# Two gaps in SBUF: weight tiles and gated activations moved to 224 bytes past a multiple of 256

## The chip, the core and the metric

The kernel runs on one core of a Trainium2 chip. The metric is the time of one execution in device microseconds (us). A run of the profiler gives, for one execution, the start and the duration of every instruction on the engines: TensorE (PE, and PEld for its weight loads), VectorE (DVE), ScalarE (ACT), GpSimd (POOL) and the queue of SyncE (SP), which issues the transfers from HBM.

## The reference

Two transformer stacks follow each other on x of 512 tokens by 1024 features, in float32. Most of the work is in the feed-forward layers and the projections:

```python
def swiglu(h, w_gu, w_d):
    g, u = jnp.split(h @ w_gu, 2, axis=-1)
    return (jax.nn.silu(g) * u) @ w_d
...
    for i in range(DEPTH):            # first block: 2 layers
        x = x + 0.5 * mx[2] * swiglu(modulate(rms_norm(x, norm_g[i, 0]), mx[0], mx[1]), ffn1_w_gu[i], ffn1_w_d[i])
        if ctx_in_layer:              # layer 0: 256 tokens of context y beside x
            y = y + 0.5 * my[2] * swiglu(modulate(rms_norm(y, norm_g[i, 0]), my[0], my[1]), ffn1_w_gu[i], ffn1_w_d[i])
...
        x = x + mx[5] * ox            # differential attention (i = 0) or Fourier mixing (i = 1)
        x = x + 0.5 * mx[8] * swiglu(modulate(rms_norm(x, norm_g[i, 2]), mx[6], mx[7]), ffn2_w_gu[i], ffn2_w_d[i])
...
    for l in range(DEPTH):            # second block: 2 layers
        mix = jnp.concatenate([o_a, o_b, o_c, o_d], axis=-1) @ w_out[l]
        h = layer_norm(DEEPNORM_ALPHA * h + mix, ln_mix_g[l], ln_mix_b[l])
        up = depthwise_conv(h @ ffn_w_up[l], ffn_conv_w[l], ffn_conv_b[l])
        f = (jax.nn.silu(up[..., :D_FF]) * up[..., D_FF:]) @ ffn_w_down[l]
        h = layer_norm(DEEPNORM_ALPHA * h + f, ln_ffn_g[l], ln_ffn_b[l])
```

The hidden width D_FF is 2816, that is 22 tiles of 128.

## The kernel before

Features lie on the 128 partitions and tokens along the free dimension, so an activation of 1024 features is a tile of 8 rows of 512 tokens in each partition. To keep float32 accuracy, every operand of a large product is split into two float32r numbers, a high and a low part, and a product is made of three matmuls: high weights by low activations, high by high, low by high. The helper `mm3` (L246 to L255) issues them, each loop of `product` one k-tile of 128 features:

```python
for pt, rh, rl in outs:
    self.PE.matmul(pt, lh, rl, start=start, stop=False)
for pt, rh, rl in outs:
    self.PE.matmul(pt, lh, rh, start=False, stop=False)
for pt, rh, rl in outs:
    last = self.PE.matmul(pt, ll, rh, start=False, stop=stop)
```

The first operand (`lh`, `ll`) is the stationary one, 128 by 128, which a weight load puts into the array; the second (`rl`, `rh`) is the moving one, which streams through it, 512 or 256 columns of 4 bytes in each partition. In a row of the profile `mm<-H,wh` the first name behind the arrow is the moving tile and the second the stationary one.

A unit of weights (512 KB, 4096 bytes in each partition) goes this way: SP issues its transfer into one of three raw tiles `wr` (L218), ACT copies it as float32r into `wh` and DVE makes the rest `wl` (L222 and L223, four tiles of each), then PE uses `wh` and `wl` for 24 matmuls or more. In the feed-forward layers the weights are stationary and the normed input `H` is moving (gate and up products), then the gated activations `ah` and `al`, which ACT and DVE split from `act` in the same way, are moving (down products, `into_stream`). In the projections that give tokens on partitions the roles are turned: `H` is stationary and `wh`, `wl` are moving. In the first feed-forward layer each matmul of 512 columns for x (bank `mm`) is followed by one of 256 columns for y (bank `my`) with the same weights. When a layer ends, the last four row blocks are made in two halves of 256 columns each, so that the norm of one half can begin during the other. In the mixers of the second block the attention scores are float32r matmuls of `q` and `k` with 512 columns (L1120, L1134 to L1136).

Nothing in the kernel chooses an address. Tiles lie in the order in which pools are opened: from the low end the pool `const`, then `weights` (`wr`, `wh`, `wl`), then `small` (tiles of 32 bytes), then the pools of a phase (`ah`, `al`, `act`, `t`, `q`, `k` and others); from the high end, on the right side, `H` and `Y`. Each tile takes its bytes in a partition, rounded up to 32. From the sizes this gives, as offsets in a partition modulo 256: `wr`, `wh`, `wl` 192 (the pool begins at 40640), `ah`, `al`, `act`, `q`, `k` and the attention outputs `Oh`, `Ol` 32 (the phases begin at 86816), `H` 224, `X` 192. Rows of a tile are whole multiples of 256 bytes apart, so all rows of one tile have its value, except for a few odd sizes in the Fourier phase.

Of the kernel before, what the change touches and what calls it, by code (L numbers as in the profile page):

```python
# [10 lines left out]
F32 = mybir.dt.float32  # L11
# [7 lines left out]
P = 128  # L19
# [45 lines left out]
class Seg:  # L65


    def __init__(self, x, lo, w, off, cond):
        self.x, self.lo, self.w, self.off, self.cond = x, lo, w, off, cond
# [103 lines left out]
class Net:  # L173
    def __init__(self, tc, a, out, ctx):
        self.tc, self.nc, self.a, self.out, self.ctx = tc, tc.nc, a, out, ctx
        nc = tc.nc
        self.V, self.S, self.G, self.PE = nc.vector, nc.scalar, nc.gpsimd, nc.tensor
        self.n = 0
        pool = lambda name, **k: ctx.enter_context(tc.tile_pool(name=name, **k))
        self.cp = pool("const", bufs=1)  # L180
        self.wp = pool("weights", bufs=1)
        self.sp = pool("small", bufs=1)
        self.fillers, self.done, self.ready = [], set(), {}
        self.steps, self.pending = 0, []

# [158 lines left out]
    def setup(self):  # L344
        nc, cp, a = self.nc, self.cp, self.a
        self.vec = cp.tile([P, NVEC], F32, name="vec")
        nc.sync.dma_start(self.vec, a["vecs"])
        self.X = cp.tile([P, KD, T], F32, name="X")
        self.ident = cp.tile([P, P], F32, name="ident")
        make_identity(nc, self.ident)  # L350
        self.ones = cp.tile([P, 2, 32], F32, name="ones")
        nc.vector.memset(self.ones, 0.0)
        for c in range(2):
            nc.vector.memset(self.ones[:, c, c:c + 1], 1.0)
        self.one2, self.ones = self.ones, self.ones[:, 0]
        self.row1 = self.one2[:, 0, :1]
        self.mhalf = cp.tile([P, 1], F32, name="mhalf")
        nc.vector.memset(self.mhalf, -0.5)
        self.eps = {e: cp.tile([P, 1], F32, name=f"eps{i}") for i, e in enumerate((1e-6, 1e-5))}
        for e, t in self.eps.items():  # L360
            nc.vector.memset(t, e)
        self.SC = cp.tile([P, KD, 32], F32, name="SC")
        nc.vector.memset(self.SC, 0.0)
        self.S.activation(self.SC[:, :, 0], self.v("c"), AF.Silu)
        self.S.activation(self.SC[:, :, 1], self.v("c_ctx"), AF.Silu)
        self.mod = [cp.tile([P, 9, KD, 2], F32, name=f"mod{l}") for l in range(2)]
        self.rows = cp.tile([P, 384], F32, name="rows")
        self.subg = cp.tile([P, 1], F32, name="subg")
        self.V.tensor_scalar(self.subg, self.v("sub_g"), 1.0 - LAMBDA_INIT, None, ALU.mult)
# [1169 lines left out]
```

## Time and profile before

| | |
|---|---|
| median of 3 runs | 3479.23 us (3478.27 to 3481.52) |
| profiled execution | 3478.89 us, span of its instructions 3477.1 us |
| mean granted TensorE clock | 0.991 of full speed |
| PE busy | 3371.0 us, 97% of the span |
| DVE, ACT, POOL busy | 1929.3, 1273.7, 318.9 us |
| from HBM | 336.82 MB, 97 GB/s over the span |

The profiled execution lies 0.34 us below the median. Matmuls are pipelined: the duration that the profile gives for one overlaps the next, so the pace of a stream of matmuls is read from starts, as the time from one start to a later one divided by the number of matmuls between them.

### The profile page before, as it was taken

What the parts mean: (1) busy time and instruction counts of PE and PEld (TensorE: products, weight loads), DVE (VectorE), ACT (ScalarE), POOL (GpSimd) and SP (SyncE); (2) the same over time, 40 slices, a digit from 0 to 9 for tenths busy, and PEclk for the clock granted to TensorE, in tenths of its full rate; (3) what the DMA queues carried; (4) which work ended last, traced back from release to release, by engine and by line L of the source; (5) the groups of instructions that cost most, each with busy time, mean ns of one, the idle gap of its engine ahead of it and who ended that gap; (6) DMA issues with size and microseconds to landing.
All of it is one profiled execution on the core that took longest, in us unless ns stands there. A gap on an engine that the chain in (4) does not pass through costs nothing.

```text
span 3477.1 us, 43820 instructions
## 1 busy us (share of the span) xinstructions
PE 3371.0 (97%) x17412; PEld 2785.0 (80%) x17412; DVE 1929.3 (55%) x2994; ACT 1273.7 (37%) x2197; POOL 318.9 (9%) x344
## 2 busy tenths in 40 slices
PE   6999999999999999999999999999999999999998
PEld 5888888777787777888888888886888888688887
DVE  6554444565855545433365333678645467865555
ACT  3212112436742222422244222445533344553333
POOL 1000000222210000100030000310100022010001
PEclk9999999999999999999999999999999999999999
DMA  6434443124235654323222322211222222023232
GB/s 214 136 112 124 131 133 98 61 72 108 58 123 175 197 160 158 101 93 93 90 88 86 96 92 93 93 52 36 86 91 91 96 92 69 25 85 94 90 100 63
DMA packets 105046, 352.51 MB, mean 101 GB/s; under 512 B 12037, under 2 KB 15237, under 8 KB 104585
## 3 DMA queue, kind: packets, MB, share of 16 engines
q1 hardware_dynamic: 104840, 349.71, 32.2%
q8 instruction: 137, 2.24, 0.3%
q14 instruction: 69, 0.56, 0.1%
HBM read 336.82 MB, written 2.10 MB: 97 GB/s over the span
## 4 chain that ended last, share of the span: by engine, by line
PE 43%; DVE 4%; ACT 1%; POOL 1%; issue 1%; DVEq 0%; ACTq 0%; POOLq 0%
PE mm L250 13%; PE mm L254 13%; PE mm L252 13%; PE tr L1144 1%; DVE ya L1252 1%; DVE nm L1121 0%; PE tr L285 0%; ACT H L222 0%; PE tr L290 0%; PE mm L1134 0%; PE mm L1153 0%; ACT X L166 0%; DVE t L164 0%; DVE t L165 0%; PE mm L1136 0%
## 5 line engine op out<-in xcount | busy, mean ns | idle before, releaser
L222 ACT ACTIVATE wh<-wr 128x1024 fp32r<-128x1024 f32 (+4 forms) x505 | 510.6, 1013 | 1397.9 <-PE mm L252 937.2
L250 PE MATMUL mm<-H,wh 128*128 128x512 f32 (+1 forms) x2592 | 970.9, 375 | 7.3 <-DVE H L138 3.0
L252 PE MATMUL mm<-H,wh 128*128 128x512 f32 (+1 forms) x2592 | 968.0, 374 | 0.0
L254 PE MATMUL mm<-H,wl 128*128 128x512 f32 (+1 forms) x2592 | 966.8, 374 | 0.2 <-DVE wl L223 0.2
L223 DVE TENSOR_TENSOR wl<-wr,wh 128x1024 fp32r<-128x1024 f32 (+4 forms) x505 | 595.7, 1182 | 472.4 <-ACT wh L222 461.5
L250 PEld LDWEIGHTS mm<-H,wh 128*128 128x128 f32 x2592 | 489.9, 189 | 107.6 <-issue 4.1
L254 PEld LDWEIGHTS mm<-H,wl 128*128 128x128 f32 x2592 | 489.5, 189 | 93.7 <-DVE wl L223 0.4
L252 PEld LDWEIGHTS mm<-H,wh 128*128 128x128 f32 x2592 | 490.5, 189 | 92.3
L250 PE MATMUL mm<-al,wh 128*128 128x512 f32 (+1 forms) x1216 | 445.0, 366 | 0.0
L252 PE MATMUL mm<-ah,wh 128*128 128x512 f32 (+1 forms) x1216 | 444.5, 366 | 0.0
L254 PE MATMUL mm<-ah,wl 128*128 128x512 f32 (+1 forms) x1216 | 443.1, 365 | 0.0
L250 PEld LDWEIGHTS mm<-al,wh 128*128 128x128 f32 x1216 | 228.2, 188 | 43.2 <-issue 1.2
L254 PEld LDWEIGHTS mm<-ah,wl 128*128 128x128 f32 x1216 | 228.7, 188 | 40.8
L252 PEld LDWEIGHTS mm<-ah,wh 128*128 128x128 f32 x1216 | 228.5, 188 | 40.1
L303 POOL TENSOR_TENSOR s<-s,mhalf 128x2 f32<-128x2 f32 (+4 forms) x70 | 77.7, 1110 | 1578.2 <-ACT s L310 815.8
L404 DVE SCALAR_TENSOR_TENSOR macc<-wr,SC,macc 128x1024 f32<-128x1024 f32 x133 | 168.5, 1281 | 90.8 <-DMA wr<-w_mod 90.2
L553 DVE SCALAR_TENSOR_TENSOR X<-mm,ng,X 128x512 f32<-128x512 f32 (+1 forms) x120 | 81.4, 678 | 246.3 <-PE mm L254 246.2
L513 DVE TENSOR_TENSOR act<-act,mm 128x512 f32<-128x512 f32 x88 | 60.4, 686 | 247.2 <-PE mm L254 247.1
L250 PE MATMUL mm<-wl,H 128*128 128x512 f32 (+2 forms) x480 | 178.2, 374 | 8.1 <-DVE wl L223 4.7
L254 PE MATMUL mm<-wh,H 128*128 128x512 f32 (+2 forms) x480 | 175.3, 367 | 0.3
L252 PE MATMUL mm<-wh,H 128*128 128x512 f32 (+2 forms) x480 | 174.9, 365 | 0.0
L222 ACT ACTIVATE ah<-act 128x512 fp32r<-128x512 f32 (+1 forms) x132 | 88.0, 667 | 161.5 <-DVE act L541 110.1
(351 smaller groups left out, 4323.4 us busy)
## 6 DMA issues: line engine op xcount, KB each, us to landing
wr<-gu SPq DMA_DIRECT2D x176, 512.0 KB, 3.5
wr<-w_mod SPq DMA_DIRECT2D x136, 512.0 KB, 4.2
wr<-up SPq DMA_DIRECT2D x88, 512.0 KB, 3.5
wr<-dn SPq DMA_DIRECT2D x48, 448.0 KB, 3.3
wr<-down SPq DMA_DIRECT2D x32, 448.0 KB, 3.3
wr<-qkv SPq DMA_DIRECT2D x24, 512.0 KB, 3.6
wr<-dn SPq DMA_DIRECT2D x24, 512.0 KB, 3.5
wr<-w_out SPq DMA_DIRECT2D x16, 512.0 KB, 3.6
```

Source lines behind the costliest of these rows:

```text
L222: self.S.activation(hi, src, AF.Copy)
L223: (eng or self.V).tensor_tensor(lo, src, hi.bitcast(F32), ALU.subtract)
L250: self.PE.matmul(pt, lh, rl, start=start, stop=False)
L252: self.PE.matmul(pt, lh, rh, start=False, stop=False)
L254: last = self.PE.matmul(pt, ll, rh, start=False, stop=stop)
L303: G.tensor_tensor(dst, v, self.mhalf.to_broadcast([P, w]), ALU.pow)
L404: self.V.scalar_tensor_tensor(acc[c], raw, s, acc[c], ALU.mult, ALU.add)
L513: self.V.tensor_tensor(to, to, pu, ALU.mult)
L553: self.V.scalar_tensor_tensor(s(d), pt, gate[0][:, d, s.cond:s.cond + 1], s(d), ALU.mult, ALU.add)
L1144: PE.matmul(d["o"], d["v"][:, t], d.pop(("p", t)), start=t == 0, stop=t == 3)
L1252: self.V.scalar_tensor_tensor(ya[:, j], ap[:, j, t:t + T], wt, ya[:, j], ALU.mult, ALU.add)
```

## The change

Two tiles are added that nothing writes or reads: one of 32 bytes in `const`, ahead of `SC`, and one of 160 bytes at the head of `small`.

```diff
@@ -180,6 +180,7 @@
         self.cp = pool("const", bufs=1)
         self.wp = pool("weights", bufs=1)
         self.sp = pool("small", bufs=1)
+        self.sp.tile([P, 40], F32, name="pad", tag="pad", bufs=1)
         self.fillers, self.done, self.ready = [], set(), {}
         self.steps, self.pending = 0, []
 
@@ -359,6 +360,7 @@
         self.eps = {e: cp.tile([P, 1], F32, name=f"eps{i}") for i, e in enumerate((1e-6, 1e-5))}
         for e, t in self.eps.items():
             nc.vector.memset(t, e)
+        cp.tile([P, 8], F32, name="gap")
         self.SC = cp.tile([P, KD, 32], F32, name="SC")
         nc.vector.memset(self.SC, 0.0)
         self.S.activation(self.SC[:, :, 0], self.v("c"), AF.Silu)
```

Everything behind `SC` in `const` and the pool `weights` move up by 32 bytes, everything from the small tiles on by 192. On every engine the same instructions stand in the same order with the same waits; only addresses differ. Offsets in a partition modulo 256:

| tiles | before | after |
|---|---|---|
| `wr`, `wh`, `wl` | 192 | 224 |
| `ah`, `al`, `act`, `q`, `k`, `Oh`, `Ol` | 32 | 224 |
| `H` (right side) | 224 | 224 |
| `X` | 192 | 192 |
| `ks`, `aT`, `pp` of the attention core | 64 | 0 |

## Rows read from the trace of the kernel before

**Rows 1.** The page, busy time: busy us (share of the span) xinstructions.

```profile
PE 3371.0 (97%) x17412; PEld 2785.0 (80%) x17412; DVE 1929.3 (55%) x2994; ACT 1273.7 (37%) x2197; POOL 318.9 (9%) x344
```

**Rows 2.** The waits: engine and line, waited for whom, us in total, times, longest.

```profile
ACT wh L222 <- PE mm L252: 938.5, 315, 5.9
```

**Rows 3.** The waits of SP's queue, in the same columns.

```profile
SPq L218 <- DVE wl L223: 2396.0, 465, 82.4
```

**Rows 4.** Groups by line and shape: xcount | busy us, mean ns | idle before, releaser.

```profile
L250 PE MATMUL mm<-H,wh 128*128 128x512 f32 x2080 | 824.0, 396 | 2.1 <-ACT wh L222 2.1
...
L222 ACT ACTIVATE wh<-wr 128x1024 fp32r<-128x1024 f32 x376 | 397.6, 1060 | 998.4 <-PE mm L252 712.1 <-PE my L252 140.0 <-DMA wr<-gu 76.8
L250 PE MATMUL mm<-al,wh 128*128 128x512 f32 x896 | 354.1, 396 | 0.0
...
L250 PE MATMUL mm<-H,wh 128*128 128x256 f32 x512 | 146.9, 290 | 5.2 <-DVE H L138 3.0 <-POOL H L223 1.7 <-DVE H L223 0.3
...
L250 PE MATMUL mm<-wl,H 128*128 128x512 f32 x320 | 127.9, 403 | 4.9 <-DVE wl L223 4.7
...
L250 PE MATMUL my<-H,wh 128*128 128x256 f32 x352 | 99.4, 282 | 0.0
...
L250 PE MATMUL mm<-al,wh 128*128 128x256 f32 x320 | 90.9, 284 | 0.0
...
L250 PE MATMUL my<-al,wh 128*128 128x256 f32 x176 | 49.3, 280 | 0.0
```

**Rows 5.** Timeline of PE, `H` moving, 512 columns: start us, us, instruction.

```profile
2000.07 0.40 PE L250 MATMUL mm<-H,wh 128*128 128x512 f32 x1
...
2039.98 0.39 PE L250 MATMUL mm<-H,wh 128*128 128x512 f32 x1
```

**Rows 6.** Timeline of PE, gated activations moving, 512 columns.

```profile
1939.88 0.40 PE L250 MATMUL mm<-al,wh 128*128 128x512 f32 x1
...
1979.78 0.40 PE L250 MATMUL mm<-al,wh 128*128 128x512 f32 x1
```

**Rows 7.** Timeline of PE, weights moving, 512 columns.

```profile
632.05 0.40 PE L250 MATMUL mm<-wl,H 128*128 128x512 f32 x1
...
659.81 0.40 PE L254 MATMUL mm<-wh,H 128*128 128x512 f32 x1
```

**Rows 8.** Timeline of PE, `H` moving, pairs of 512 and 256 columns.

```profile
364.77 0.39 PE L254 MATMUL mm<-H,wl 128*128 128x512 f32 x1
...
394.93 0.39 PE L254 MATMUL mm<-H,wl 128*128 128x512 f32 x1
```

**Rows 9.** Timeline of PE, gated activations moving, pairs of 512 and 256 columns.

```profile
314.76 0.39 PE L250 MATMUL mm<-al,wh 128*128 128x512 f32 x1
...
344.86 0.39 PE L254 MATMUL mm<-ah,wl 128*128 128x512 f32 x1
```

**Rows 10.** Timeline of PE, gated activations moving, 256 columns.

```profile
1375.85 0.29 PE L252 MATMUL mm<-ah,wh 128*128 128x256 f32 x1
...
1386.41 0.28 PE L254 MATMUL mm<-ah,wl 128*128 128x256 f32 x1
```

**Rows 11.** Timeline of PE, `H` moving, 256 columns, in two layers.

```profile
1403.87 0.28 PE L254 MATMUL mm<-H,wl 128*128 128x256 f32 x1
...
1419.96 0.28 PE L252 MATMUL mm<-H,wh 128*128 128x256 f32 x1
...
1851.84 0.28 PE L250 MATMUL mm<-H,wh 128*128 128x256 f32 x1
...
1869.96 0.28 PE L252 MATMUL mm<-H,wh 128*128 128x256 f32 x1
```

**Rows 12.** Timeline of PE, attention scores of the two mixers, 512 columns.

```profile
2386.76 0.40 PE L1134 MATMUL mm<-q,k 128*128 128x512 f32 x1
...
2388.14 0.38 PE L285 MATMUL tr<-ident,nm 128*128 128x128 f32 x2
...
3006.66 0.40 PE L1134 MATMUL mm<-q,k 128*128 128x512 f32 x1
...
3008.05 0.38 PE L285 MATMUL tr<-ident,nm 128*128 128x128 f32 x2
```

## The prediction

> **What bounds the kernel now.** I read the busy times first, because a change of addresses alone can only act through the durations of instructions and transfers. PE is busy 97% of the span [rows 1], so a change in the pace of its matmuls reaches the end nearly whole. Next come the waits, to see whether the feeders have room. ACT, which starts the split of each weight unit, stands 938.5 us waiting for PE to give back a `wh` tile [rows 2], and the queue that issues the weight transfers waits 2396.0 us for DVE to give back a raw tile [rows 3]. Both are ahead of PE, so a split or a transfer that became some per cent slower would be covered, and a faster PE is still fed.
>
> Then the groups by shape give the counts. `mm3` issues three matmuls a k-tile, on three lines with equal counts, so each L250 row stands for three. With 512 columns these are 3 × 2080 = 6240 with `H` moving, 3 × 896 = 2688 with the gated activations moving and 3 × 320 = 960 with weights moving. With 256 columns they are 3 × 512 = 1536 with `H` and 3 × 320 = 960 with gated activations, besides 3 × 352 = 1056 and 3 × 176 = 528 in bank `my`, nearly all of which follow a 512-column matmul as the second of a pair [rows 4].
>
> Last, the pace, from starts in the timeline. This is the reading that the whole forecast hangs on, since operands at different offsets modulo 256 already stand beside each other in this trace. I write (moving, stationary) for the two offsets.
> - 512 columns, (224, 192): 171 matmuls in 39.91 us, 233.4 ns each [rows 5].
> - 512 columns, (32, 192): 171 in 39.90 us, 233.3 ns [rows 6].
> - 512 columns, (192, 224): 119 in 27.76 us, 233.3 ns [rows 7].
> - Pairs of 512 and 256, (224, 192): 87 pairs in 30.16 us, 346.7 ns [rows 8]; (32, 192): 86 pairs in 30.10 us, 350.0 ns [rows 9].
> - 256 columns, (32, 192): 88 in 10.56 us, 120.0 ns [rows 10]; (224, 192): 138 in 16.09 us, 116.6 ns, but elsewhere 151 in 18.12 us, 120.0 ns [rows 11].
> - 512 columns, (32, 32), the only place where both operands have one offset: 6 in 1.38 us and 6 in 1.39 us, together 230.8 ns [rows 12].
>
> Two things are to be seen. Pace does depend on something besides the column count: 3.3 ns, or 8 ticks of 2.4 GHz, come and go. And the three plain streams of 512 columns, the bulk of the run, agree to 0.1 ns at three moving offsets, so the moving address by itself does nothing to them; only the scores with equal offsets run faster, by 2.5 ns.
>
> **The change part by part.** Instructions, order and waits are unchanged, so no term comes from a moved wait. The change has these pieces.
>
> *Gated activations from 32 to 224.* If they then behave as `H` does at 224, each of the 528 pairs gains 350.0 − 346.7 = 3.3 ns, 1.7 us. Each of the 960 matmuls of 256 columns gains between 0 and 120.0 − 116.6 = 3.4 ns, since `H` shows both paces; I take 2 ns, 1.9 us (bounds 0 and 3.3 us).
>
> *Weights from 192 to 224, under `H` and the gated activations at 224.* Both operands now have one offset in all big products. No row shows (224, 224). The nearest for equal offsets is the scores' 230.8 ns, the nearest for 224 with another partner is 233.4 ns. So a plain 512-column matmul gains between 0 and 2.5 ns. I take 2.5, because equal offsets are the nearer likeness: stream of the same type, same length, one variable changed. Counting all of bank `my` as pairs, plain ones are 6240 − 1056 = 5184, 2688 − 528 = 2160 and 960: 8304 × 2.5 ns = 20.8 us. On the other side, equal offsets might be the ones that collide; then a matmul loses the same quantum, 3.3 ns, which I keep for the rivals. For `H` in pairs and in 256 columns I take nothing, as they already show the lower pace in places.
>
> A rule of the Trainium skill speaks against this term. The page "TensorE: Matmul & The Clock Gate", section "Step-by-step: what each phase is for", says that PE reads the streaming operand and the next weights through two independent ports, so that loading weights takes nothing from the running matmul. By it the offset of the weights could not matter, the term would be zero, and the sum would be the one of the rival "only the moving address". The trace agrees as far as the 192 and 224 of plain streams go and disagrees in the scores, if those are slowed or sped by nothing else.
>
> *Splits on ACT and DVE, transfers into `wr`.* Their addresses move too. A split of 1024 elements takes ACT 1060 ns [rows 4]; were every one 5% slower, 376 × 53 ns = 20 us would fall into the 938.5 us that ACT waits anyway. A unit's matmuls take 24 × 0.2333 = 5.6 us, and the transfers wait for raw tiles. I cost these at nothing; without that cover it would be up to the 20 us.
>
> *Attention core (64 to 0), small tiles, `mod`, `rows`.* No matmul stream of weight; nothing.
>
> Sum: 20.8 + 1.7 + 1.9 = 24.4 us. The profiled execution's 3478.89 − 24.4 = 3454.5; the median lies 0.34 above it, so 3455 us.
>
> **The rivals.**
> *Only the moving address counts.* For it: the three equal paces of 512 columns, and that the scores come in short runs between other work, so that their 230.8 ns rest on a dozen starts. Against it: those starts repeat in both mixers within 1.7 ns. It leaves 1.7 us of pairs and up to 3.3 us of 256 columns: 3479.2 − 5.0 = 3474 us, a gain of 0.14%, below the 0.2% (7 us) that a measurement of this kernel can tell from no change.
>
> *Nothing depends on addresses.* The change then doesn't do what its offsets suggest: the 3.3 ns belong to where a stream begins, as the two paces of `H` at one and the same offset hint [rows 11]. 3479 us.
>
> *Equal offsets collide: slower.* With both operands of every product walking through the same 256 bytes in step, weight load and stream could meet in the same part of the memory. Place: all products. Price: the quantum of 3.3 ns on each of the 8304 plain ones (27.4 us), and on `H`'s 1056 pairs and 1536 matmuls of 256 columns, which lose what they now have (8.6 us): 3479 + 36 = 3515 us. It decides as soon as a plain matmul takes 0.84 ns more (7 us / 8304). Against it: the scores have equal offsets and are not slower.
>
> **How the numbers follow.** Chances: equal offsets faster 0.50, only the moving address 0.25, nothing 0.12, collision 0.13. The likeliest gives 3455 us; its own range goes from the whole quantum of 3.3 ns on the 8304 plain matmuls, on `H`'s pairs and 256 columns (27.4 + 8.6) and the 5.0 us of the gated activations, −41 us, 3438, to 1.5 ns a plain matmul with the pairs, −14 us, 3465. To leave out no more than the collision, the range takes in the first and second rivals: 3438 to 3482. Faster by over 0.2% means below 3472: 0.50 and a sliver of the first rival, 0.52. Within 0.2%: 0.35. Slower: 0.13.
>
> **What would show it right or wrong.** In the timeline after, plain 512-column matmuls should start every 230.8 ns (8 × 3 of them a unit, 5.54 us in place of 5.60) with `H`, with `ah` and `al`, and with weights moving alike; pairs with `ah` at 346.7 ns, as those with `H`; 256 columns of `ah` below 120 ns. Means of ACT's and DVE's splits should stay within 1%. 233.3 ns in all plain streams with pairs at 346.7 would speak for the moving address alone; pairs of `ah` still at 350.0 for no effect; anything over 234.2 ns for a collision. I am wrong, above all, if the scores' pace comes from their short runs and not from their offsets.

## Result, and the profile after

The changed kernel takes 3442.3 us (median of 4 runs, 3435.44 to 3443.33) against 3480.38 us before: a ratio of 0.9884, 95% interval 0.9869 to 0.99, so 38 us or 1.2% faster. The profiled execution of the changed kernel took 3443.33 us, its span is 3441.5 us.

The busy line of the page after, which answers to [rows 1]:

```profile
PE 3336.6 (97%) x17412; PEld 2795.6 (81%) x17412; DVE 1929.3 (56%) x2994; ACT 1274.0 (37%) x2197; POOL 320.1 (9%) x344
```

Every engine has the same number of instructions. PE's busy time fell by 34.4 us; that of its weight loads (PEld), which overlap the matmuls, rose by 10.6 us, and the other three engines stayed within 1.2 us. The wait of ACT for a `wh` tile, [rows 2], fell from 938.5 to this (the waits of the changed kernel; its lines are one or two lower down than before):

```profile
ACT wh L223 <- PE mm L253: 882.2, 314, 4.7
```

So the faster PE took its time out of ACT's slack and was still fed. The means of the splits did not move (1060 ns for ACT's, as in [rows 4]).

The timeline of PE after, at the same instructions as [rows 5 to 12] with one stretch of pairs added. Two rows are the first and the last start of a stretch:

```profile
314.13 0.39 PE L251 MATMUL mm<-al,wh 128*128 128x512 f32 x1
...
343.95 0.39 PE L255 MATMUL mm<-ah,wl 128*128 128x512 f32 x1
...
363.71 0.39 PE L255 MATMUL mm<-H,wl 128*128 128x512 f32 x1
...
393.87 0.39 PE L255 MATMUL mm<-H,wl 128*128 128x512 f32 x1
...
411.16 0.40 PE L253 MATMUL mm<-H,wh 128*128 128x512 f32 x1
...
442.61 0.40 PE L251 MATMUL mm<-H,wh 128*128 128x512 f32 x1
...
632.75 0.40 PE L251 MATMUL mm<-wl,H 128*128 128x512 f32 x1
...
659.75 0.39 PE L255 MATMUL mm<-wh,H 128*128 128x512 f32 x1
...
1399.21 0.28 PE L255 MATMUL mm<-H,wl 128*128 128x256 f32 x1
...
1415.77 0.28 PE L253 MATMUL mm<-H,wh 128*128 128x256 f32 x1
...
1922.94 0.39 PE L251 MATMUL mm<-al,wh 128*128 128x512 f32 x1
...
1961.70 0.39 PE L251 MATMUL mm<-al,wh 128*128 128x512 f32 x1
...
1981.42 0.39 PE L251 MATMUL mm<-H,wh 128*128 128x512 f32 x1
...
2020.18 0.39 PE L251 MATMUL mm<-H,wh 128*128 128x512 f32 x1
...
2365.21 0.39 PE L1136 MATMUL mm<-q,k 128*128 128x512 f32 x1
...
2366.60 0.38 PE L286 MATMUL tr<-ident,nm 128*128 128x128 f32 x2
```

Read as before, start to start:

| stream | matmuls between the rows | before, ns | after, ns |
|---|---|---|---|
| 512 columns, `H` moving | 171 | 233.4 | 38.76 us / 171 = 226.7 |
| 512 columns, `al`, `ah` moving | 171 | 233.3 | 226.7 |
| 512 columns, weights moving | 119 | 233.3 | 226.9 |
| pairs, `ah` and `al` | 86 pairs | 350.0 | 346.7 |
| pairs, `H`, at 364 us | 87 pairs | 346.7 | 346.7 |
| pairs, `H`, at 411 us | 89 pairs | 346.7 | 353.4 |
| 256 columns, `H`, at 1399 us | 138 | 116.6 | 120.0 |
| scores, 512 columns | 6 | 230.8 | 231.7 |

The plain streams of 512 columns, three kinds of operands alike, are 6.6 ns faster, not 2.5. The 256 columns of `H` are slower, and so is about half of the pairs of `H`.

PE's 17412 matmul records stand in the same order in both traces, so the time from each start to the next can be subtracted one by one. With the starts that a wait or the lower clock delayed put apart as gaps, the 35.6 us between the spans (3477.1 and 3441.5) come out as: plain 512 columns −51.7 us; 256 columns +3.9; pairs +2.5; gaps +8.4; and PE's first matmul starts 1.4 us later.

### The profile page after: what moved, and what is told of

The parts are those of the page before. It is cut to its first block, busy times and chain, and to the rows that moved or that the text cites. A ratio compares the mean times of both kernels' runs of the same rounds, so it can differ in the third digit from the quotient of the medians.

```text
span 3441.5 us, 43820 instructions
## 1 busy us (share of the span) xinstructions
PE 3336.6 (97%) x17412; PEld 2795.6 (81%) x17412; DVE 1929.3 (56%) x2994; ACT 1274.0 (37%) x2197; POOL 320.1 (9%) x344
## 4 chain that ended last, share of the span: by engine, by line
PE 42%; DVE 4%; ACT 2%; POOL 1%; issue 1%; DVEq 0%; ACTq 0%; POOLq 0%
PE mm L251 13%; PE mm L255 13%; PE mm L253 13%; PE tr L1146 1%; DVE ya L1254 1%; DVE wl L224 1%; PE tr L286 0%; PE mm L1136 0%; ACT H L223 0%; PE mm L1155 0%; DVE nm L1123 0%; DVE t L164 0%; DVE t L165 0%; PE tr L291 0%; PE mm L1138 0%
## 5 line engine op out<-in xcount | busy, mean ns | idle before, releaser
L251 PEld LDWEIGHTS mm<-al,wh 128*128 128x128 f32 x1216 | 229.5, 189 | 39.0 <-DVE al L224 1.6
L255 PEld LDWEIGHTS mm<-ah,wl 128*128 128x128 f32 x1216 | 229.5, 189 | 35.5
L253 PEld LDWEIGHTS mm<-ah,wh 128*128 128x128 f32 x1216 | 229.5, 189 | 35.4
```

## Experiments

The first theory, called theory 1 below, is that the pace of a stream hangs on the difference between the offsets of its two operands, moving less stationary, modulo 256. The rivals are named in the expectations.

**map: every pair of offsets by itself.** Eight moving and eight stationary tiles, 32 bytes apart from one to the next, each combination with 512 and with 256 columns:

```python
for kind in ("mv", "st"):
    for j in range(8):
        t = sp.tile([P, 2, T], F32R, name=kind + "ABCDEFGH"[j])
        ...
        sp.tile([P, 8], F32, name=f"{kind}gap{j}")
...
for w in (512, 256):
    for m in tiles["mv"]:
        for s in tiles["st"]:
            stream(m, s, w)          # 48 matmuls, 24 in each of two banks
```

> This kernel leaves out the whole network: it loads x, copies it into eight moving and eight stationary tiles that begin at 160, 192, 224, 0, 32, 64, 96 and 128 modulo 256, and runs for each of the 64 combinations 48 float32r matmuls back to back, first with 512 columns, then with 256. Theory 1, only the difference of the two offsets counts, and equal ones are best: the diagonal at 226.7 ns (512 columns) and 120.0 ns (256), as the changed kernel shows for (224, 224), and the other combinations equal along each diagonal, 233.3 ns at differences 32, 96 and 224. Theory 2, 224 itself is the good place: only combinations with 224 in one operand or both are at 226.7, the rest of the diagonal is at 233.3. Theory 3, the pace comes from the kernel around the matmuls and not from offsets: all 64 alike.

Offsets are A 160, B 192, C 224, D 0, E 32, F 64, G 96, H 128. Its timeline, one row for 24 matmuls; a stretch's pace is the distance to the next row, divided by 24:

```profile
125.00 5.61 PE L39 MATMUL pb<-mvB,stB 128*128 128x512 f32 x24
130.45 5.76 PE L39 MATMUL pa<-mvB,stC 128*128 128x512 f32 x24
136.04 5.76 PE L39 MATMUL pb<-mvB,stC 128*128 128x512 f32 x24
141.64 5.76 PE L39 MATMUL pa<-mvB,stD 128*128 128x512 f32 x24
...
726.38 5.61 PE L39 MATMUL pb<-mvH,stH 128*128 128x512 f32 x24
731.83 3.03 PE L39 MATMUL pa<-mvA,stA 128*128 128x256 f32 x24
```

`mvB` over `stB` takes 5.45 us, over `stC`, 32 bytes further, 5.60 us (233.3 ns); `mvH` over `stH`, at another offset, again 5.45 us. From single starts, without the first six of each combination, which settle:

| moving less stationary, bytes | 0 | 32 | 64 | 96 | 128 | 160 | 192 | 224 |
|---|---|---|---|---|---|---|---|---|
| 512 columns, ns | 226.7 | 233.2 | 228.8 | 233.3 | 232.5 | 234.4 | 233.4 | 233.4 |
| 256 columns, ns | 120.0 | 117.6 | 117.8 | 120.0 | 118.7 | 118.0 | 116.6 | 118.3 |

Each figure is a mean over the eight combinations with that difference (for 0 with 512 columns over seven, since the very first ran at the start). With 512 columns the eight agree to 0.3 ns, but for one at 128, which keeps 233.2 where the other seven have 232.4. So for 512 columns theory 1 holds and the other two fall. With 256 columns the means hide that the eight do not agree at three of the differences: at 32 there are 116.7 and 117.8 ns, at 160 117.3 and 120.0, at 192 two at 113.3 and six at 117.8. The difference alone thus does not set the pace of 256 columns, as by_width and map3 below confirm. The map also explains what the trace of before could not tell: its plain streams had the differences 32, 96 and 224, all at 233.2 to 233.4 ns.

**weights_only: half of the change.** Weights at 224, as `H` is, but gated activations at 64:

```diff
+        cp.tile([P, 8], F32, name="gap")
```

> The gap in const alone: weights at 224, H at 224, gated activations at 64 (so their difference to the weights stays the 96 of before). Theory 1 (equal offsets): streams with H and with weights moving at 226.7 ns, streams of the gated activations at 233.3 as before; of the 8304 plain matmuls 6144 gain, 74%, so about 28 of the 37 us: 3452 us. Theory 2 (the moving operand must lie at 224): nothing gained for H, which was there already; weights moving, 960 of them, gain 6 us: 3474 us.

Measured: 3451.9 us (3443.94 to 3463.43, 4 runs), ratio 0.9913, 0.989 to 0.9936. Its timeline of PE, 171 matmuls of 512 columns with `al` and 171 with `H`:

```profile
1931.82 0.40 PE L250 MATMUL mm<-al,wh 128*128 128x512 f32 x1
...
1971.73 0.39 PE L250 MATMUL mm<-al,wh 128*128 128x512 f32 x1
...
1991.59 0.39 PE L250 MATMUL mm<-H,wh 128*128 128x512 f32 x1
...
2030.35 0.39 PE L250 MATMUL mm<-H,wh 128*128 128x512 f32 x1
```

`al`, at a difference of 96, stays at 39.91 / 171 = 233.4 ns; `H`, whose own address did not move, goes to 226.7. The weights' address alone does it. The four runs spread over 19.5 us, so it is the paces that carry this, and not how near the median came to 3452.

**acts_only: the other half.** Gated activations at 224, weights left at 192:

```diff
+        self.sp.tile([P, 48], F32, name="pad", tag="pad", bufs=1)
```

> The pad in small alone, of 192 bytes: gated activations and H at 224, weights at 192. Theory 1: no product has equal offsets, the gated activations now do what H did before: 233.3 ns plain, 346.7 in pairs: 2 to 5 us gained, 3475 to 3478 us. Theory 2: streams of the gated activations, 2160 plain matmuls, go to 226.7: 14 us gained, 3466 us.

Measured: 3478.73 us (10 runs), ratio 0.999, 0.9979 to 1.0001: no more than a hint of a gain. In its trace all pairs of the gated activations run at 346.7 ns, their 256 columns at 116.7 and their 512 columns still at 233.3. So the two small terms of the prediction were real for this half of the change: 460 × 3.3 + 960 × 3.2 ns are 4.6 us, and the ratio stands for 3.5 us.

**all_192: equal offsets elsewhere.** All at 192 instead of 224, by a pad on the right side ahead of `H` and one ahead of the small tiles:

```diff
+        self.sp.tile([P, 40], F32, name="pad", tag="pad", bufs=1)
...
+        rp = ctx.enter_context(tc.tile_pool(name="rpad", bufs=1, side="right"))
+        rp.tile([P, 8], F32, name="rpad")
```

> All three at 192 in place of 224: 32 bytes at the right end move H to 192, 160 bytes in small move the gated activations to 192, the weights stay at 192. Theory 1: as the changed kernel, 226.7 ns everywhere, 3442 us. Theory 2: as before or worse, 233.3 ns, 3480 us.

Measured: 3443.11 us (3435.68 to 3444.44, 4 runs), ratio 0.9881, 0.9866 to 0.9896: the time of the changed kernel, and 226.7 ns in all three kinds of plain streams. There is nothing in 224 as such.

This run settles another point. Its profiled execution took 3435.68 us, 7.65 us less than that of the changed kernel, at the same paces. The stretches of the two mixers, window by window (length, busy times and counts of the engines, granted clock), first in the changed kernel, then here:

```profile
2197.20:2417.40 220.20, 213.21 (x1051) 165.42 (x1050) 173.14 (x401) 112.94 (x248) 41.09 (x48) 0.97 0.18 57
2811.20:3032.10 220.90, 214.12 (x1051) 166.72 (x1050) 172.77 (x401) 112.30 (x248) 40.08 (x48) 0.96 0.17 56
```

```profile
2197.70:2413.80 216.10, 209.72 (x1049) 162.86 (x1048) 172.84 (x400) 112.56 (x248) 40.80 (x48) 0.98 0.18 58
2807.80:3024.80 217.00, 210.77 (x1048) 164.02 (x1048) 172.62 (x400) 112.00 (x248) 39.86 (x48) 0.98 0.18 57
```

The mixers take 8.0 us less here, at a granted clock of 0.98 in place of 0.97 and 0.96; a mean below 1 is a part of the stretch at 1.2 GHz. Before the change they took 217.8 and 216.2 us at 0.99 and 1.00. In the control further below, again with all offsets equal, the same instructions take 216.1 and 216.9 us. So equal offsets do not by themselves cost the mixers their clock, and both kernels have runs near 3435 and near 3443 us; why one execution loses more than another is not shown.

**map2: single bytes, pairs and short runs.** The stationary tile fixed, the moving one 0 to 96 bytes past it in small steps; pairs of 512 and 256 columns; runs of five matmuls between others.

```python
fine = [moving("mv" + "ABCDEFGHIJKL"[i], d) for i, d in
        enumerate((0, 1, 2, 4, 6, 8, 10, 12, 16, 18, 20, 24))]     # floats
```

> Leaves out the network as the first map did. One stationary tile at 128 modulo 256, twelve moving tiles 0, 4, 8, 16, 24, 32, 40, 48, 64, 72, 80 and 96 bytes further, streams of 48 matmuls each with 512 and then with 256 columns; then streams of 48 pairs of 512 and 256 columns for differences 0, 32, 64, 96, 128, 160, 192 and 224; then twelve runs of five 512-column matmuls at equal offsets, each followed by two small float32 matmuls. Theory A, the two reads meet in pieces of 32 bytes, so that only the difference in steps of 32 counts: 226.7 ns for 0 to 24 bytes, 233.3 for 32 to 48, 228.8 for 64 to 80, 233.3 for 96. Theory B, single bytes count: 226.7 at 0 alone and another pace at 4 bytes already. Pairs: 350 ns at difference 0, 346.7 at 32 and 350.0 at 96, as the three layouts of the kernel show. Short runs at equal offsets: about 231 ns for the first five, as the scores, if a stream needs some matmuls to find its steady pace; 226.7 from the first if the scores are slow for another reason.

| difference, bytes | 0 | 4 | 8 | 16 | 24 | 32 | 48 | 64 | 96 |
|---|---|---|---|---|---|---|---|---|---|
| 512 columns, ns | 227.5 | 236.7 | 231.7 | 231.8 | 235.1 | 233.4 | 230.0 | 228.9 | 233.3 |
| 256 columns, ns | 120.0 | 123.4 | 116.7 | 113.3 | 120.1 | 116.6 | 118.4 | 117.8 | 119.9 |
| pairs, ns | 353.2 | | | | | 346.7 | | 353.4 | 350.0 |

Theory B holds, down to one float: 4 bytes take the best pace of 512 columns to the worst. (The stream at 0 is the kernel's first, and 227.5 still holds some of its start; its last 30 matmuls run at 226.7.) The pairs answer for the first feed-forward layer: 346.7 at 32 and 350.0 at 96, the two paces of [rows 8, 9]. At 0 they run at 353.2 and not at the 350 expected, which is about the mean of the two paces that the changed kernel has there. One of the runs of five at equal offsets, and the start of what comes behind it:

```profile
350.16 1.39 PE L52 MATMUL pa<-mvA,st 128*128 128x512 f32 x5
351.39 0.60 PE L54 MATMUL pb<-X 128*128 128x128 f32 x4
```

The first of the five, straight behind the float32 matmuls, takes 314 ns to the next start; the other four take 227 to 232, 229.5 on average, where the long stream ends at 226.7. So a stream first settles, and that is most of what sets the 230.8 ns of the scores apart from 226.7; the last nanosecond is not accounted for.

**by_width and its control.** Since one offset cannot suit 512 columns, 256 columns and pairs, the weight tiles are made 256 bytes wider and each use places its weights in them; a pad of 192 bytes, as in acts_only, puts the gated activations at 224:

```diff
+FULL, NARROW, PAIR = 8, 4, 0
...
-        return [self.wp.tile([P, 1024], F32R, name=self.nm(t), tag=t, bufs=4) for t in ("wh", "wl")]
+        return [self.wp.tile([P, 1088], F32R, name=self.nm(t), tag=t, bufs=4)[:, self.off:self.off + 1024] for t in ("wh", "wl")]
...
+                self.off = NARROW if split else FULL if len(parts) == 1 else PAIR
...
-                        net.phase(c, "proj", 6)
+                        net.phase(c, "proj", 5)
```

The control has all three at 8 floats.

> The whole network. Control for the next kernel: weight tiles are 256 bytes wider than they need be, and every product reads them 32 bytes into the tile, so that all stand at 224, as the moving tiles do (difference 0, as in the changed kernel); the projection phase has five buffers for its tile t in place of six, to make room. Theory 1 (the pace hangs on the difference alone): plain streams of 512 columns at 226.7 ns, of 256 columns at 120.0, pairs near 349 to 350; the time of the changed kernel, 3442 us, ratio 0.988 to 0.990. Rival (the fifth buffer or the wider tiles cost something): more than 3450 us.

> The whole network. The weight tiles are read at an offset that suits the columns of the stream: 224 (difference 0) for plain streams of 512, 208 (moving operand 16 bytes past the stationary one) for streams of 256 alone, 192 (difference 32) for the pairs of 512 and 256 in the first feed-forward layer. Theory 1 (the paces measured by themselves hold in the network): 226.7 ns, 113.3 ns and 346.7 ns; 2844 matmuls of 256 columns gain 6.7 ns each (19 us), some 930 pairs with H 3.5 ns and 445 with the gated activations 1.8 ns (4 us) against the control, so about 3419 us, ratio 0.982. Rival (in the network the streams of 256 columns do not reach the pace, as they are cut by waits and by the clock): 116 to 120 ns, 3428 to 3440 us, ratio 0.985 to 0.988. Second rival (the gain goes into more stretches at the low clock): the paces are there and the time is still within 0.2% of the control.

Measured: the control 3438.66 us (3436.83 to 3440.34, 4 runs), ratio 0.9874, 0.9859 to 0.9889, so the wider tiles and the fifth buffer cost nothing that shows; by width 3431.41 us (3431.0 to 3433.79, 4 runs), ratio 0.9855, 0.9838 to 0.9872. The runs do not overlap: 7 us less, a third of the 23 that theory 1 gave. All pairs have 346.7 ns, and by the subtraction used above that gives the 4 us expected of them. But the streams of 256 columns did not come to 113.3. Two of them in the timeline, 116 matmuls and 93:

```profile
1836.04 0.28 PE L255 MATMUL mm<-H,wh 128*128 128x256 f32 x1
...
1849.96 0.28 PE L255 MATMUL mm<-H,wh 128*128 128x256 f32 x1
...
2411.01 0.28 PE L257 MATMUL mm<-H,wh 128*128 128x256 f32 x1
...
2421.92 0.28 PE L257 MATMUL mm<-H,wh 128*128 128x256 f32 x1
```

13.92 / 116 = 120.0 ns and 10.91 / 93 = 117.3 ns, both at a difference of 16, without a wait in them. Each stream keeps one of the two for its whole length. The first rival's figures came (116 to 120 ns, 3428 to 3440 us), but not for its reason, since no wait or lower clock cuts these two streams. The pace of 256 columns is not a function of the difference alone, and theory 1 was too simple.

**map3 and by_width_192: what picks the rhythm.** Streams of 48 matmuls with 256 columns at four differences, with something else ahead of each (at a difference of 0 the two float32 matmuls ran at the very start instead):

```python
for m in fine:                        # 0, 16, 32, 192 bytes past the stationary tile
    for how in range(8):
        before(how)                   # nothing, 2 of float32, or 7 to 12 matmuls of 128, 384 or 512 columns
        stream(m, N, 256)
```

> The network is left out (the output is no result of it); 32 streams of 48 matmuls with 256 columns, at four differences (moving offset less stationary offset, modulo 256): 0, 16, 32 and 192 bytes, eight streams of each. The eight differ only in the few matmuls that stand ahead of them: none, two of 128 columns in float32, or short float32r streams of 7 to 12 matmuls with 512, 384 or 128 columns. Theory M (at one difference there are several steady rhythms, and what ran just before picks one): at 16 the eight streams do not agree, paces of 113.3, 117.3 and 120.0 ns turn up among them, at 32 116.7, 117.8 and 120.0, while at 0 all eight settle at 120.0. Rival (the network's other traffic in SBUF disturbs the streams): here, where nothing else runs, all eight of a difference agree, 113.3 at 16 and 116.7 at 32.

Three of its streams, one at 0 (`mvA`) and two at 16 (`mvB`); each lasts to the start in the row behind it:

```profile
65.99 5.92 PE L40 MATMUL pa<-mvA,st 128*128 128x256 f32 x48
71.75 2.29 PE L40 MATMUL pb<-mvD,st 128*128 128x384 f32 x12
...
99.61 5.61 PE L40 MATMUL pa<-mvB,st 128*128 128x256 f32 x48
105.06 1.73 PE L40 MATMUL pb<-mvA,st 128*128 128x384 f32 x9
...
113.13 5.92 PE L40 MATMUL pa<-mvB,st 128*128 128x256 f32 x48
118.89 2.72 PE L40 MATMUL pb<-mvC,st 128*128 128x512 f32 x11
```

The stream at 0 takes 5.76 us, 120.0 ns a matmul; at 16 the same 48 matmuls take 5.45 or 5.76 us. From the last 33 starts of each: at 0 all eight streams run at 120.0 ns; at 16 two at 113.3, four at 116.7 and two at 118.7; at 32 six at 116.7 and two at 117.8; at 192 three at 113.3 and five at 117.8. Nothing else runs here, so the rival (disturbance by the network's traffic) falls: there are several rhythms at one difference. The expected set was not exact, since 118.7 came in place of 117.3 and 120.0.

That what ran just before picks the rhythm is not shown by map3 alone, where each way of starting ran once at each difference. The traces of the network bear it out. Cut into 50 blocks of 24 pairs, the changed kernel, all_192 and the control, all with equal offsets, have the same pace (346.7 or 353.3 ns) in 47 of them, so the choice repeats from execution to execution. In weights_only `H` and the weights lie as in the changed kernel and only the gated activations, which run in between, are at another difference: there ten blocks of `H` that have 353.3 in the changed kernel have 346.7.

The last kernel puts the 256 columns at 192 (`NARROW = 24`).

> The whole network, as the version by width, but streams of 256 columns alone read their weights at offset 32, so that the moving operand stands 192 past them in place of 16. In the map by itself 192 gave 116.6 and 113.3 ns, and one small stream of the network that stands at that difference (Vv moving) runs at 113.7. Theory M: at 192 all rhythms lie between 113.3 and 116.7, so 2844 matmuls gain 1.8 to 5.2 ns against the 118.5 of the version by width, 5 to 15 us: 3417 to 3426 us, ratio 0.981 to 0.984. Rival (a slow rhythm of 120 exists at 192 as well): no gain or a small loss, 3429 to 3436 us, ratio 0.985 to 0.987.

Measured: 3431.63 us (3431.52 to 3434.09, 4 runs), ratio 0.9853, 0.9837 to 0.987. One of its streams, 132 matmuls:

```profile
1840.04 0.28 PE L259 MATMUL mm<-H,wl 128*128 128x256 f32 x1
...
1855.00 0.28 PE L255 MATMUL mm<-H,wh 128*128 128x256 f32 x1
```

113.3 ns here, 117.8 in about half of the others, so both rhythms of map3 are there and none of 120. By the same subtraction as above its matmuls of 256 columns take 7.4 us less than those of the version by width, and yet the time is the same: gaps, at the small products of the first stage and around the streams themselves, are 7.0 us longer. Neither theory gave this time with this pace. (The 116.6 ns that the expectation took from the map is the mean of six streams at 117.8 and two at 113.3.)

Part of the gaps has nothing to do with the streams. The first matmul of 256 columns with `H` starts here, in the version by width and then in this one:

```profile
38.98 0.58 PE L255 MATMUL mm<-H,wh 128*128 128x256 f32 x1 [3.03 <-DVE H L141]
```

```profile
41.80 0.58 PE L255 MATMUL mm<-H,wh 128*128 128x256 f32 x1 [3.03 <-DVE H L141]
```

So 2.8 us were lost before any stream that the offset changes. In the eight traces of the whole network this start lies anywhere from 38.98 to 42.28 us. Between 36 and 100 us this execution also had a granted clock of 0.87 in place of 0.95, and by 120 us it is 4.6 us behind. The ratios of the two versions, each against its own runs of before, are uncertain by 0.0017 either way, about 6 us, so a gain of 7 us could not be told from none. The rest of the gaps is not settled.

## Why the prediction was right, and where it was not

**That PE's pace reaches the end, and the feeders keep up** was right: PE stayed at 97%, and ACT still waits 882.2 us for PE.

**That equal offsets make the plain 512 columns faster** was right, and weights_only, all_192 and the map show that it is the difference of the two offsets. **Its size was wrong**: 2.5 ns were taken, as the upper end, and the runs show 6.6. The step that failed is the likeness to the scores. Their 230.8 ns, which hardly changed [rows 12], come from runs of five or six matmuls, which have not settled; map2 shows the like, 229.5 against 226.7 ns, with nothing else around. The text named the short runs as what would make it wrong, but only towards no effect. The term of 20.8 us was in truth 51.7.

**"For `H` in pairs and in 256 columns I take nothing"** was wrong. Both lost: the 256 columns of `H` had 117.3 ns on average and now have 119.9 (1494 matmuls outside of gaps, 3.8 us), since a difference of 32 has faster rhythms than 120 and a difference of 0 has only that. Of 937 pairs with `H` 507 now run at 353.3 in place of 346.7 ns (3.4 us). The rival of a collision was thus right in sign for these two shapes, and wrong for the one that fills the run.

**The gated activations' two terms** (1.7 and 1.9 us) came in acts_only, as 1.5 and 3.1, and hardly here, because the weights moved too: 120 of the 460 pairs fell to 353.4 and their 256 columns stayed at 119.8, so together they gave 0.8 us.

**Splits and transfers at nothing** was right. What was not foreseen is that some of the gain came back as gaps on PE, 8.4 us in sum. A part can be named. In the second feed-forward layer the modulation vectors for later layers are made between the products: PE transposes a tile `t` that DVE has to copy out first (in `mod_out`). The wait, before and after, in the windows 1005.6 to 1397.3 us and 1004.8 to 1392.6 us:

```profile
PE tr L418 <- DVE t L415: 5.7, 4, 3.1
```

```profile
PE tr L420 <- DVE t L417: 9.4, 6, 2.3
```

DVE is busy in these windows as long as it was (219.7 and 219.4 us), and PE comes to its result earlier: that takes 3.7 us of what the streams gained there. The same wait in the other kernels, between 1000 and 1400 us, goes with the pace: 6.2 us in acts_only, whose plain streams kept theirs, 9.8 in weights_only, 11.6 in the control and 13.5 in all_192. The two mixers lost 7.1 us in this execution (434.0 to 441.1 us), at the lower granted clock told of at all_192. The other gaps together were shorter than before.

So the time came out 13 us below 3455, inside the range: a term more than twice too small, less losses that were set to nothing, and gaps. That it lies inside is in part luck: the range ended at a gain of 3.3 ns for each plain matmul, and 51.7 us with the two small terms would alone have made 3424 us, below its end of 3438.

The rule weighed in the prediction (the Trainium skill, "TensorE: Matmul & The Clock Gate", "Step-by-step: what each phase is for": streaming operand and weights are read through two independent ports) does not hold here in what the prediction drew from it, that the offset of the weights could not matter. By weights_only the weights' address alone changes a stream of `H` from 233.4 to 226.7 ns, and in the map a moving tile at 192 runs at 227 or 233.3 ns as the stationary one lies 0 or 32 bytes from it.

Why the pace hangs on the difference of the offsets is not shown by these runs, not even that the two reads meet somewhere; and neither is why a long stream keeps one of its rhythms.

## What to carry to other kernels

Where a kernel is a stream of matmuls, the difference of the two operands' offsets in a partition is a parameter that was worth 3% of a 512-column matmul here, and a pad of some bytes sets it; measure it for each column count in use, since what is best for 512 is not for 256 or for pairs. Read a pace from long streams, and never size one from runs of five or six matmuls. And count the stretches that the change makes worse, not only the one that it is for.

## What was not expected of the hardware

- One float more between the operands, 4 bytes, changes a stream of 512 columns from 227.5 to 236.7 ns (map2). Of the differences tried the best and the worst are neighbours.
- Streams of 256 columns and of pairs at one difference have several steady rhythms and stay in the one that they fall into: 113.3, 116.7 and 118.7 ns at 16 bytes (map3), and 346.7 and 353.3 ns for pairs at equal offsets (the changed kernel). With 256 columns at equal offsets all streams settled at 120.0.
